# Second layer's attention: all of the first head's weights formed beside the projection, in the room of its raw weights; cached keys loaded a block ahead

## The chip, the cores and the metric

The kernel runs on one core of one Trainium2 chip, in one launch. The metric is the device time in microseconds (us); smaller is better. Before the change the median of three runs is 2865.79 us (2862.54 to 2874.33).

The core's engines are TensorE (PE, matmuls and transposes), VectorE (DVE), ScalarE (ACT) and GpSimd (POOL). SP issues nearly all DMAs here, one after the other. Each engine's instructions run in the order in which the program lists them for that engine, each with the semaphores that it waits for; what stands behind a waiting instruction on its engine waits with it.

## The reference

One step of a streaming encoder for two groups of requests that share weights: a new stream of 16 learned rows and 1024 frames (the prompt), and 32 further frames of a running stream (the sample) with 1024 rows of cache. Two layers, each with a mixer and an MLP of 4096, width 1024, all in float32. The second layer's mixer is forgetting attention with 16 heads of 64:

```python
q, k, v, fl = split_cols(h @ w_in, C_SIZES)          # 1024, 1024, 1024, 16 columns
q = rmsnorm(q.reshape(B_, L, H_C, HEAD_DIM), qn)     # per head
k = rmsnorm(k.reshape(B_, L, H_C, HEAD_DIM), kn)
logf = jax.nn.log_sigmoid((fl + b_f).astype(jnp.float32))
...
s = einsum('bqhd,bkhd->bhqk', q, k) * SCALE + c[q] - c[k]   # c: running sum of logf
p = softmax(where(kpos <= qpos, s, NEG))
o = einsum('bhqk,bkhd->bqhd', p, v)
```

The sample's rows do the same against the 1024 cached keys and values and their own 32. Each output of the projection (new keys, new values, logf) is also an output of the kernel.

## The kernel before, in words

**Precision.** A float32 operand is split into a high part, which TensorE takes at its fast float32 rate, and the rest. `hi_lo` (L62 to L68) does it: a cast on ACT (L64), a subtraction on DVE (L66) or POOL (L68). `mm3` (L71 to L77) then makes a product from three matmuls (high by high, high by low, low by high).

**The end of the first layer.** The MLP of layer 0 ends at about 1324 us in the trace. The norm ahead of the second mixer is computed for four quarters of the 1056 rows; the first three are done inside the MLP, the last stands behind it in the program: squares on ACT (L134), their sums on DVE and POOL (L136, L139), a matmul with the mean (L145), ACT and DVE for the reciprocal root (L148 to L152), the scaling of eight blocks on DVE (L217), and the splitting of each block into high and low (L64, L66, L68), the low part on DVE and POOL by turns. Its scratch tiles live in a pool that is closed directly after (`nms.close()`). Then the pool `fh0` opens, which holds what belongs to head 0 of the attention.

**The projection** (`project_c`, with `project`, L230 to L269): seven groups of columns, one after the other; for each, four loads of raw weights (two blocks of 128 input rows each, L240), their split into `pj_wh` and `pj_wl`, and then nine tiles of rows, each 8 x 3 matmuls into one bank of PSUM. That makes 63 steps. What a step leaves is normed, transposed (L1177) and written to DRAM (`zq`, `zk`, `zv`). The raw weights have a tile of their own, `pj_raw`, three buffers.

**Work beside the projection.** A table gives what is emitted behind which step: behind step 45 the loads of head 0's queries, keys and values (`head_load`, L1418), and behind 56, 58, 60 and 62 its first four blocks of scores with their softmax (`head_scores` L1438, `softmax` L1270). A block of scores is a high matmul (L1452), a low one (L1453) and a mask (L1456), in pieces of a bank's 512 columns or in a wider tile `fx_s`; block number j has 16 + 128 (j + 1) columns. The softmax takes the maximum on DVE (L1275), the exponential on ACT (L1279), and normalises on POOL (L1283). The weights stay in `fx_p0` (four short blocks) and `fx_p1` (six buffers, long blocks).

**The attention** (`fox`, L1487 on): the order on PE is written out by hand. A unit is a head and half of its queries; a step transposes one block of weights (`head_weights`, L1470) and multiplies the values (`head_values`, L1480, L1481); a table sets at which step of head h the scores of head h + 1 are formed, and for head 0 the last four scores are formed beside its first four steps. The sample's attention (`fox_sample`) goes between: per group of four heads, two blocks of 512 cached keys (`fk_c`, loaded at L1318, transposed at L1322), scores (L1334, L1335), cached values. The other engines' order, and SP's order of DMA issues, is set by a scheduler that simulates a timeline.

Of the kernel before, what the change touches and what calls it, by code (L numbers as in the profile page):

```python
# [8 lines left out]
F32 = mybir.dt.float32  # L9
# [9 lines left out]
P = 128  # L19
# [32 lines left out]
class Core:  # L52
# [177 lines left out]
    def project(self, w, cols, sb, hT, lag, part, width=512, bufs=(3, 5)):  # L230
# [3 lines left out]
        for n, (a, b, post, bank) in enumerate(cols):  # L234
            ws = []
            for k in range(0, KB, 2):
                raw = sb.tile([P, 2, width], F32, name="pj_raw", bufs=bufs[0])
# [921 lines left out]
    def project_c(self, hT, beside):  # L1159
        tc, nc, i, o = self.tc, self.nc, self.i, self.o  # L1160
        with tc.tile_pool(name="pc", bufs=2, reuse_waits="tile") as sb, tc.tile_pool(name="pcp", bufs=4, space=PSUM, reuse_waits="tile") as ps:
# [33 lines left out]
            def post_v(h0, nh, gates):  # L1195
                def post(t, r0, m, pp):
# [6 lines left out]
                    if gates:  # L1203
# [30 lines left out]
                                 lambda: sb.tile([P, 512], F32, name="hn_sq"), bufs=(3, 4))  # L1234
            for n, _ in enumerate(steps):
# [3 lines left out]
                if n in beside:  # L1239
                    beside[n]()  # L1240


    def forget_sums(self, sb):
# [9 lines left out]
        for dst, parts in ((self.cp, prompt), (self.cs, sample)):  # L1253
# [9 lines left out]
            for a in range(0, n, n // 2):  # L1263
                hl = [sb.tile([16, 528], F32R, name=f"fs_{x}")[:, :n // 2] for x in "hl"]
                self.hi_lo(d[:, a:a + n // 2], *hl)
                for x in range(2):
                    nc.sync.dma_start(dst[x, :, a:a + n // 2], hl[x].bitcast(F32))


    def softmax(self, sb, pieces, p, n):  # L1270
        nc = self.nc
        nm = sb.tile([P, 2], F32, name="sm_nm", bufs=4)
        den = sb.tile([P, 2], F32, name="sm_den", bufs=4)
        for j, (s, a, b) in enumerate(pieces):
            nc.vector.tensor_reduce(nm[:, j:j + 1], s, axis=AX.X, op=ALU.max, negate=True)  # L1275
        if len(pieces) == 2:
            nc.vector.tensor_tensor(nm[:, 0:1], nm[:, 0:1], nm[:, 1:2], op=ALU.min)
        for j, (s, a, b) in enumerate(pieces):
            nc.scalar.activation(p[:, a:b], s, AF.Exp, bias=nm[:, 0:1], accum_out=den[:, j:j + 1])  # L1279
        if len(pieces) == 2:  # L1280
            nc.vector.tensor_tensor(den[:, 0:1], den[:, 0:1], den[:, 1:2], op=ALU.add)
# [5 lines left out]
    def fox_sample(self, sb, work, ms):  # L1287
# [15 lines left out]

        def keys(g, a, p):
            def go():
# [132 lines left out]
    def head_scores(self, qi, d, sb, ps=None):  # L1438
# [19 lines left out]
        p = sb.tile([P, 1040], F32, name="fx_p1", bufs=6) if qi > 3 else self.fh0.tile([P, 528], F32, name="fx_p0", bufs=4)  # L1458
# [25 lines left out]
    def fox(self, d0, p0, ms, norm):  # L1484
        tc, nc, i = self.tc, self.nc, self.i
        w = i["w_out_c"][0]
        with ExitStack() as st:  # L1487
# [3 lines left out]
            with tc.tile_pool(name="fh", bufs=2, reuse_waits="tile") as sb, tc.manual_schedule(engines={mybir.EngineType.PE}):  # L1491
# [16 lines left out]
                d, pr = {0: d0}, {(0, 0): p0}  # L1508
# [49 lines left out]
                for u, (h, quad) in enumerate(units):  # L1558
                    for t in range(4 * quad + 5):
                        step = 5 * quad + t  # L1560
                        if h == 14 and step == 0:
                            for n, names in enumerate((("fk_c", "fk_h", "fk_l"), ("fx_s", "fx_cs", "fv_c"))):
                                raw, wh, wo = (ssb.tile([P, 2, 512], F32R if x else F32, name=y, bufs=1) for x, y in enumerate(names))
# [3 lines left out]
                        if h == 0 and step < 4:  # L1567
                            scores(0, 4 + step)
# [39 lines left out]
def body(tc, i, o):  # L1608
    C = Core(tc, i, o)
    nc = tc.nc  # L1610
    with ExitStack() as st:
# [109 lines left out]
        with tc.tile_pool(name="fh0", bufs=1, reuse_waits="tile") as fh0:  # L1721
            C.fh0 = fh0
# [103 lines left out]
```

## Time and profile before

| what | before |
|---|---|
| median of three runs | 2865.79 us (2862.54 to 2874.33) |
| profiled execution, its own time | 2855.66 us |
| its span | 2853.9 us |
| PE busy | 2631.2 us, 92% |
| DVE / ACT / POOL busy | 1888.3 / 1264.4 / 560.7 us |
| mean granted clock of PE | 0.963 |
| DMA | 393.77 MB, 138 GB/s on average |
| matmuls of the third projection | 1326.71 to 1643.04 us |

All rows of the trace are from the one profiled execution, in microseconds from its start. The span is the time from its first to its last instruction; 1.8 us of its time lie around that. "Busy" is the sum of the durations of an engine's instructions; "granted clock" is the share of TensorE's full clock that it got in that stretch (1.00 is all of it). In a row of instructions the bracket tells how long the engine was idle before it, and which instruction ended that.

### The profile page before, as it was taken

The page shows a single profiled execution, that of the slowest core. Times are in us where ns is not written, and L with a number is a line of the kernel's source. Part 1 is how long each engine was busy: PE and PEld are TensorE (multiplying, and loading weights), DVE is VectorE, ACT ScalarE, POOL GpSimd, SP SyncE. Part 2 cuts the span into 40 slices and gives each one's busy share as a digit, 9 for nine tenths or more (in the row PEclk, how much of TensorE's full clock was granted, in tenths as well). Part 3 has the DMA queues.
Part 4 walks back from the last instruction along what each step waited for, and adds up shares of the span by engine and source line. Part 5 has one row for each costly group of instructions (what it writes and reads, how often), then busy time and mean ns, then how long its engine had stood idle before and what let it go on. Part 6 is the DMA issues. An engine that isn't in the chain of part 4 may idle for free.

```text
span 2853.9 us, 49119 instructions
## 1 busy us (share of the span) xinstructions
PE 2631.2 (92%) x18391; PEld 2440.6 (86%) x18391; DVE 1888.3 (66%) x3856; ACT 1264.4 (44%) x2820; POOL 560.7 (20%) x611
## 2 busy tenths in 40 slices
PE   5899988879999899999999978999978999899998
PEld 5788966769999799999789856778768999899998
DVE  5934376687676677578643556778888666677553
ACT  4435454243333345445333346666653333335342
POOL 3423354200000010003110244555520000010000
PEclk9999988899999899999999979999988999999999
DMA  5343241143445577544465374344332444486643
GB/s 192 100 134 104 72 140 45 30 120 101 151 129 164 202 231 218 168 134 121 123 193 168 115 176 127 89 101 102 77 91 79 144 147 144 164 274 205 200 138 105
DMA packets 371286, 393.77 MB, mean 138 GB/s; under 512 B 41503, under 2 KB 300280, under 8 KB 369000
## 3 DMA queue, kind: packets, MB, share of 16 engines
q1 hardware_dynamic: 368552, 383.62, 45.6%
q0 software_dynamic: 2496, 7.01, 0.7%
q8 instruction: 145, 2.38, 0.4%
q14 instruction: 93, 0.76, 0.1%
HBM read 263.94 MB, written 125.48 MB: 136 GB/s over the span
## 4 chain that ended last, share of the span: by engine, by line
PE 63%; issue 16%; DVE 9%; DMA 3%; ACT 2%; SPq 1%; POOL 1%; DVEq 0%; ACTq 0%; POOLq 0%
PE bank L75 11%; PE bank L76 11%; PE bank L77 11%; PE mu_y L77 5%; PE mu_y L76 5%; PE mu_y L75 5%; PE bank L1470 2%; PE bank L1480 1%; PE bank L1481 1%; PE fx_s L1452 1%; PE fx_s L1453 1%; DMA md_raw<-in_w_down 1%; PE bank L257 1%; DVE gl_Q L600 1%; PE b L701 1%
## 5 line engine op out<-in xcount | busy, mean ns | idle before, releaser
L75 PE MATMUL bank<-pj_wh,h 128*128 128x384 f32 (+3 forms) x832 | 298.0, 360 | 9.4 <-ACT pj_wh L64 7.0
L77 PE MATMUL bank<-pj_wh,h 128*128 128x384 f32 (+3 forms) x832 | 295.9, 357 | 6.0 <-DVE h L66 4.8
L76 PE MATMUL bank<-pj_wl,h 128*128 128x384 f32 (+3 forms) x832 | 297.3, 358 | 3.5 <-DVE pj_wl L66 3.5
L75 PE MATMUL mu_y<-md_u,md_w 128*128 128x268 f32 (+1 forms) x896 | 259.4, 289 | 26.9 <-ACT md_u L64 26.9
L76 PE MATMUL mu_y<-md_u,md_w 128*128 128x268 f32 (+1 forms) x896 | 257.8, 288 | 2.4 <-DVE md_u L66 2.4
L77 PE MATMUL mu_y<-md_u,md_w 128*128 128x268 f32 (+1 forms) x896 | 257.3, 287 | 0.0
L75 PE MATMUL bank<-md_u,md_w 128*128 128x268 f32 (+1 forms) x896 | 257.1, 287 | 0.0
L77 PE MATMUL bank<-md_u,md_w 128*128 128x268 f32 (+1 forms) x896 | 255.2, 285 | 0.0
L76 PE MATMUL bank<-md_u,md_w 128*128 128x268 f32 (+1 forms) x896 | 254.9, 285 | 0.0
L64 ACT CAST md_u<-md_ur 128x536 fp32r<-128x536 f32 (+1 forms) x224 | 141.1, 635 | 210.7 <-PE mu_y L77 110.7
L66 DVE TENSOR_TENSOR md_u<-md_ur,md_u 128x536 fp32r<-128x536 f32 (+1 forms) x224 | 157.9, 710 | 114.2 <-ACT md_u L64 113.8
L76 PE MATMUL mu_y<-ho_T,mu_w 128*128 128x268 f32 (+1 forms) x768 | 219.8, 286 | 0.2 <-DVE ho_T L66 0.2
L77 PE MATMUL mu_y<-ho_T,mu_w 128*128 128x268 f32 (+1 forms) x768 | 219.9, 286 | 0.0
L75 PE MATMUL mu_y<-ho_T,mu_w 128*128 128x268 f32 (+1 forms) x768 | 219.2, 285 | 0.0
L75 PEld LDWEIGHTS mu_y<-md_u,md_w 128*128 128x128 f32 x896 | 171.1, 191 | 27.4 <-ACT md_u L64 27.3
L66 DVE TENSOR_TENSOR mu_w<-mu_raw,mu_w 128x512 fp32r<-128x512 f32 x160 | 110.0, 688 | 117.0 <-ACT mu_w L64 117.0
L1283 POOL TENSOR_TENSOR fx_p<-fx_p,sm_den 128x144 f32<-128x144 f32 (+7 forms) x128 | 150.6, 1177 | 181.8 <-DVE sm_den L1282 164.7
L64 ACT CAST mu_w<-mu_raw 128x512 fp32r<-128x512 f32 x160 | 99.2, 622 | 188.6 <-PE bank L77 124.6
L75 PEld LDWEIGHTS bank<-pj_wh,h 128*128 128x128 f32 x832 | 158.8, 191 | 22.3 <-ACT pj_wh L64 7.5
L76 PEld LDWEIGHTS mu_y<-md_u,md_w 128*128 128x128 f32 x896 | 170.9, 191 | 3.5 <-DVE md_u L66 3.4
L77 PEld LDWEIGHTS bank<-pj_wh,h 128*128 128x128 f32 x832 | 158.6, 191 | 17.5 <-DVE h L66 5.1
L76 PEld LDWEIGHTS bank<-pj_wl,h 128*128 128x128 f32 x832 | 159.0, 191 | 16.3 <-DVE pj_wl L66 5.2
(538 smaller groups left out, 8096.2 us busy)
## 6 DMA issues: line engine op xcount, KB each, us to landing
md_raw<-in_w_down SPq DMA_DIRECT2D x160, 256.0 KB
mu_raw<-in_w_up SPq DMA_DIRECT2D x64, 512.0 KB
ud<-xT SPq DMA_DIRECT2D x16, 1876.0 KB
md_ur<-ud SPq DMA_DIRECT2D x112, 268.0 KB
ud<-xT SPq DMA_DIRECT2D x16, 1848.0 KB
md_ur<-ud SPq DMA_DIRECT2D x112, 264.0 KB
md_k<-in_w_down SPq DMA_DIRECT2D x16, 1024.0 KB
fh_ka<-zk SPq DMA_DIRECT2D x32, 260.0 KB
```

What stands on the lines that cost most here:

```text
L64: nc.scalar.copy(hi, src)
L66: nc.vector.tensor_tensor(lo, src, hi.bitcast(F32), op=ALU.subtract)
L75: mm(out, ah, bh, start=start, stop=False)
L76: mm(out, ah, bl, start=False, stop=False)
L77: mm(out, al, bh, start=False, stop=stop)
L257: nc.tensor.matmul(*args, start=k == x == 0, stop=k == KB - 1 and x == 1)
L600: eng.tensor_tensor(ov, xv[r, :, :, 1], qv[r, :, :, 1], op=ALU.mult)
L701: nc.tensor.matmul(po[:m, h % 2, h // 2], att[:, h, :m], v[:, P * h:P * h + P], start=True, stop=False)
L1283: nc.gpsimd.tensor_tensor(p[:, :n], p[:, :n], den[:, 0:1].to_broadcast([P, n]), op=ALU.mult)
L1452: nc.tensor.matmul(s[:, a:b], qa[:, qc], ka[:, t0 + a:t0 + b], start=True, stop=False)
L1453: nc.tensor.matmul(s[:, a:b], qb[:, qc], kb[:, t0 + a:t0 + b], start=False, stop=ma >= mb)
L1470: nc.tensor.transpose(pt[:m, P * j:P * j + P], pr[j][:, k0:k0 + m], self.ident)
```

## The change

- `project` may take its raw weights' buffers from outside. The third projection now uses four buffers of head 0's pool (`fx_p10` to `fx_p13`, 1040 columns wide, 1024 used), taken by turns, in place of its own three. The same four buffers then hold head 0's long blocks of weights.
- All eight of head 0's blocks of scores are formed beside the projection, behind steps 50, 52, 54, 55, 57, 59, 61 and 62. The softmax takes up to three pieces for that, since the longest block needs three banks. `fox` no longer forms any of head 0's scores.
- The running sums of the forget gate are split and written in quarters (264 columns) instead of halves, with a smaller tile.
- The block of cached keys is loaded one block ahead, into two buffers; the first load is issued when `fox_sample` begins.

```diff
@@ project
-                raw = sb.tile([P, 2, width], F32, name="pj_raw", bufs=bufs[0])
+                raw = raws() if raws else sb.tile([P, 2, width], F32, name="pj_raw", bufs=bufs[0])
@@ project_c
-                                 lambda: sb.tile([P, 512], F32, name="hn_sq"), bufs=(3, 4))
+                                 lambda: sb.tile([P, 512], F32, name="hn_sq"), bufs=(3, 4),
+                                 raws=lambda: self.weights_tile(self.fh0)[:, 0:1024].rearrange("p (k n) -> p k n", k=2))
+    def weights_tile(self, sb):
+        j = self.turn % (4 if sb is self.fh0 else 6)
+        self.turn += 1
+        return (self.fh0 if j < 4 else sb).tile([P, 1040], F32, name=f"fx_p1{j}", bufs=1)
@@ forget_sums
-            for a in range(0, n, n // 2):
-                hl = [sb.tile([16, 528], F32R, name=f"fs_{x}")[:, :n // 2] for x in "hl"]
-                self.hi_lo(d[:, a:a + n // 2], *hl)
+            for a in range(0, n, n // 4):
+                hl = [sb.tile([16, 264], F32R, name=f"fs_{x}")[:, :n // 4] for x in "hl"]
+                self.hi_lo(d[:, a:a + n // 4], *hl)
                 for x in range(2):
-                    nc.sync.dma_start(dst[x, :, a:a + n // 2], hl[x].bitcast(F32))
+                    nc.sync.dma_start(dst[x, :, a:a + n // 4], hl[x].bitcast(F32))
@@ softmax
-        nm = sb.tile([P, 2], F32, name="sm_nm", bufs=4)
-        den = sb.tile([P, 2], F32, name="sm_den", bufs=4)
+        nm = sb.tile([P, 3], F32, name="sm_nm", bufs=4)
+        den = sb.tile([P, 3], F32, name="sm_den", bufs=4)
...
-        if len(pieces) == 2:
-            nc.vector.tensor_tensor(nm[:, 0:1], nm[:, 0:1], nm[:, 1:2], op=ALU.min)
+        for j in range(1, len(pieces)):
+            nc.vector.tensor_tensor(nm[:, 0:1], nm[:, 0:1], nm[:, j:j + 1], op=ALU.min)
...
@@ fox_sample
+        def cached(g, a):
+            kc = sb.tile([P, 4, 256], F32, name="fk_c", bufs=2)
+            nc.sync.dma_start(kc, i["cache_c_k"][0, 0, 512 * a:512 * a + 512, 4 * g:4 * g + 4].rearrange("(n p) h d -> p n (h d)", p=P))
+            return kc
+
+        ahead = [cached(0, 0)]
...
                 if p == 0:
-                    kc = st["kc"] = sb.tile([P, 4, 256], F32, name="fk_c", bufs=1)
-                    nc.sync.dma_start(kc, i["cache_c_k"][0, 0, 512 * a:512 * a + 512, h0:h0 + 4].rearrange("(n p) h d -> p n (h d)", p=P))
+                    st["kc"] = ahead.pop()
+                    if g + a < 4:
+                        ahead.append(cached(g + a, 1 - a))
@@ head_scores
-        p = sb.tile([P, 1040], F32, name="fx_p1", bufs=6) if qi > 3 else self.fh0.tile([P, 528], F32, name="fx_p0", bufs=4)
+        p = self.weights_tile(sb) if qi > 3 else self.fh0.tile([P, 528], F32, name="fx_p0", bufs=4)
@@ fox
-                d, pr = {0: d0}, {(0, 0): p0}
+                d, pr = {0: d0}, {(0, 0): p0[:4], (0, 1): p0[4:]}
+                self.turn = 4
...
-                        if h == 0 and step < 4:
-                            scores(0, 4 + step)
@@ body
-            C.fh0 = fh0
+            C.fh0, C.turn = fh0, 0
...
-                                  **{56 + 2 * q: lambda q=q: p0.append(C.head_scores(q, d0, fh0)) for q in range(4)}})
+                                  **{n: lambda q=q: p0.append(C.head_scores(q, d0, fh0)) for q, n in enumerate((50, 52, 54, 55, 57, 59, 61, 62))}})
```

How the instructions moved is seen at three places. The rows give the line, the operation, what is written and read, the size of what is written and, in brackets, the semaphores that the instruction waits for: `PE`, `DVE`, `Pool` and `Activation` are raised by those engines, `DMAHW` and `DMASW` by earlier DMAs.

The first is SP at the start of the projection. `md_ur` is the last load of the MLP, `fs_cache` the cached forget gates. Before:

```order
L1058 DMA md_ur<-ud_6543 128x2x268 [waits DMAHW3_49,DVE_49]
L240 DMA pj_raw<-in_w_in_c 128x2x272 [waits PE_49] x2
L240 DMA pj_raw<-in_w_in_c 128x2x272
L1248 DMA fs_cache<-in_cache_c_logf 128x8x16 [waits DVE_49,PE_49]
L240 DMA pj_raw<-in_w_in_c 128x2x272 [waits DMAHW7_49,DVE_49]
```

and of the change:

```order
L1058 DMA md_ur<-ud_6543 128x2x268 [waits DMAHW3_49,DVE_49]
L1255 DMA fs_cache<-in_cache_c_logf 128x8x16 [waits DVE_49,PE_49]
L240 DMA fx_p_14497<-in_w_in_c 128x2x272 [waits DVE_49,PE_49,Pool_49]
L240 DMA fx_p_14503<-in_w_in_c 128x2x272 [waits DVE_49,Pool_49]
L240 DMA fx_p_14509<-in_w_in_c 128x2x272
L240 DMA fx_p_14515<-in_w_in_c 128x2x272
```

The four loads of the first column group now stand behind `fs_cache`, go to the `fx_p` buffers, and the first two wait for DVE and POOL. In the built program the values waited for are those of the last norm's writes of `h`: for the first load DVE's low part of the fifth block and POOL's of the sixth, for the second load DVE's of the seventh and POOL's of the eighth. The buffers lie where the norm's scratch pool was.

The second is PE behind the projection's last matmuls. `L1177` is the transpose of a projected tile, `fh_ka`/`fh_kb` and `fh_qa` are head 0's keys and queries, `fx_p` its weights. Before:

```order
L1177 MATMUL bank<-ident,pc_z 128x128 x4
L1452 MATMUL fx_s<-fh_ka,fh_qa 128x512
L1453 MATMUL fx_s<-fh_kb,fh_qb 128x512
L1452 MATMUL fx_s<-fh_ka,fh_qa 128x144
L1453 MATMUL fx_s<-fh_kb,fh_qb 128x144
L1456 LDWEIGHTS identb
L1456 MATMUL fx_s<-causal,identb 128x128
L1177 MATMUL bank<-ident,pc_z 128x128 x4
L1452 MATMUL bank<-fh_ka,fh_qa 128x512
```

and of the change:

```order
L1177 MATMUL bank<-ident,pc_z 128x128 x4
L1467 MATMUL bank<-fh_ka,fh_qa 128x512
L1468 MATMUL bank<-fh_kb,fh_qb 128x512
L1467 MATMUL bank<-fh_ka,fh_qa 128x400
L1468 MATMUL bank<-fh_kb,fh_qb 128x400
L1471 LDWEIGHTS identb
L1471 MATMUL bank<-causal,identb 128x128
L1177 MATMUL bank<-ident,pc_z 128x128 x4
L1467 MATMUL bank<-fh_ka,fh_qa 128x512
L1468 MATMUL bank<-fh_kb,fh_qb 128x512
L1467 MATMUL bank<-fh_ka,fh_qa 128x512
```

Between the last two tiles' transposes stood score block 4 (656 columns), behind them block 3 and then 5, 6 and 7 among the first weights' transposes; now it is block 6 (912 columns) and then block 7 (1040), and blocks 3, 4 and 5 are ahead of the last projection matmul.

The third is SP ahead of the first block of cached keys. Before (of the eight `fq_s` loads one is shown; head 2's loads stood four rows behind the `fk_c`):

```order
L1294 DMA fx_oc<-in_c_sel 8x128 [waits DMAHW0_49]
L1298 DMA fx_mh<-zk_77 128x8x32 [waits DMAHW1_49,DMASW4_49,DMASW3_49]
L1298 DMA fx_ml<-zk_77 128x8x32 [waits DMAHW2_49]
L1309 DMA fx_cs<-cs 4x1056 [waits DMAHW3_49]
L1314 DMA fq_s<-zq_76 64x32 [waits DMAHW4_49,Pool_49]
...
L1318 DMA fk_c<-in_cache_c_k 128x4x256 [waits DMAHW5_49,PE_49]
```

and of the change:

```order
L1447 DMA fh_qa<-zq_76 64x1024 [waits DMAHW0_49,PE_49]
L1447 DMA fh_qa<-zq_76 64x1024 [waits DMAHW1_49]
L1447 DMA fh_ka<-zk_77 64x1040 [waits DMAHW2_49]
L1447 DMA fh_ka<-zk_77 64x1040 [waits DMAHW3_49]
L1447 DMA fh_qb<-zq_76 64x1024 [waits DMAHW4_49,PE_49]
L1301 DMA fx_oc<-in_c_sel 8x128 [waits DMAHW7_49,DMAHW6_49,DMAHW5_49]
L1305 DMA fx_mh<-zk_77 128x8x32 [waits DMASW4_49,DMASW3_49]
L1305 DMA fx_ml<-zk_77 128x8x32
L1313 DMA fk_c<-in_cache_c_k 128x4x256 [waits DMAHW0_49]
L1323 DMA fx_cs<-cs 4x1056 [waits DMAHW1_49]
```

Five of the loads of head 2 (into head 0's buffers, so behind head 0's last scores on PE) now stand ahead of the first cached block; the samples' queries (`fq_s`) stand behind it, and the second cached block directly behind those.

More of the change, by code (lines that the diff above doesn't have):

```diff
@@ L226, in scaled, with project @@
         return to
-    def project(self, w, cols, sb, hT, lag, part, width=512, bufs=(3, 5)):
+    def project(self, w, cols, sb, hT, lag, part, width=512, bufs=(3, 5), raws=None):
         nc = self.nc
@@ L1562, in fox @@
                             for n, names in enumerate((("fk_c", "fk_h", "fk_l"), ("fx_s", "fx_cs", "fv_c"))):
-                                raw, wh, wo = (ssb.tile([P, 2, 512], F32R if x else F32, name=y, bufs=1) for x, y in enumerate(names))
+                                raw, wh, wo = (ssb.tile([P, 2, 512], F32R if x else F32, name=y, bufs=1 + (y == "fk_c")) for x, y in enumerate(names))
                                 nc.sync.dma_start(raw, w.rearrange("(k p) n -> p k n", p=P)[:, 6:8, 512 * n:512 * n + 512])
```

4 lines of the change are left out of this document (2 added, 2 removed).

## The prediction

> **What bounds the kernel now.** I read the page first (TensorE, PE below, is busy 92% of the span), then the stretches around the third projection, PE's waits there, its rows in order of time, and the chain of waits. First the stretches; the columns are the stretch and its length, then busy time with the instruction count of PE, weight loads, DVE, ACT and POOL, then granted clock, DMA share and GB/s.
>
> ```profile
> 1320.00:1340.00 20.00, 18.09 (x141) 17.57 (x141) 14.76 (x37) 11.23 (x31) 6.80 (x10) 1.00 0.49 140
> 1400.00:1420.00 20.00, 20.00 (x93) 16.41 (x92) 15.02 (x30) 8.79 (x15) 5.34 (x5) 0.96 0.72 201
> 1600.00:1640.00 40.00, 40.00 (x191) 31.90 (x190) 22.35 (x60) 12.74 (x35) 10.10 (x9) 1.00 0.45 137
> 1640.00:1700.00 60.00, 42.27 (x200) 31.44 (x199) 29.51 (x64) 27.11 (x64) 21.96 (x21) 0.74 0.63 159
> 1671.00:1674.00 3.00, 3.00 (x16) 2.77 (x15) 0.90 (x2) 1.86 (x4) 2.11 (x3) 0.50 1.08 281
> 1682.00:1688.00 6.00, 5.67 (x21) 4.19 (x22) 1.47 (x3) 1.36 (x3) 0.00 (x0) 0.50 0.18 58
> ```
>
> Inside the projection PE has no free time (40.00 of 40), so nothing that only makes room there shortens it. The two edges are different: at 1320 PE is nearly full although a norm is still being computed, and after 1640 it is busy for 42.27 of 60 us at a mean clock of 0.74. What it waits for there, in total, times and longest:
>
> ```profile
> PE bank L1322 <- DMA fk_c<-in_cache_c_k: 7.5, 2, 4.1
> PE bank L1177 <- POOL pc_z L1189: 4.2, 1, 4.2
> PE bank L1470 <- POOL fx_p L1283: 4.2, 1, 4.2
> PE fx_s L1452 <- ACT fx_p L1279: 1.7, 2, 1.4
> ```
>
> Four causes, 17.6 us. In PE's own rows (start, duration, what; the bracket is the idle time before it):
>
> ```profile
> 1326.71 0.52 PE L75 MATMUL bank<-pj_wh,h 128*128 128x272 f32 x2 [1.91 <-ACT pj_wh L64]
> ...
> 1643.04 0.60 PE L1177 MATMUL bank<-ident,pc_z 128*128 128x128 f32 x4
> 1643.39 0.48 PE L1452 MATMUL fx_s<-fh_ka,fh_qa 128*128 128x512 f32 x1
> ...
> 1644.12 0.23 PE L1456 MATMUL fx_s<-causal,identb 128*128 128x128 bf16 x1
> 1648.54 1.12 PE L1177 MATMUL bank<-ident,pc_z 128*128 128x128 f32 x4 [4.19 <-POOL pc_z L1189]
> ...
> 1670.66 1.09 PE L1322 MATMUL bank<-ident,fk_c 128*128 128x128 f32 x4 [4.12 <-DMA fk_c<-in_cache_c_k]
> ...
> 1682.33 1.08 PE L1322 MATMUL bank<-ident,fk_c 128*128 128x128 f32 x4 [3.40 <-DMA fk_c<-in_cache_c_k]
> ```
>
> The projection's matmuls run from 1326.71 to 1643.04 (called E below); E to the second block of cached keys is 39.3 us. The change acts on both ends of this.
>
> **The start of the projection: a new wait.** Before, the raw weights have their own three buffers, and three loads leave SP long before they are needed; the fourth is the one that shows what a late load costs:
>
> ```profile
> 1311.49 3.85 SPq L240 DMA_DIRECT2D pj_raw<-in_w_in_c  x3
> 1327.44 0.37 SPq L240 DMA_DIRECT2D pj_raw<-in_w_in_c  x1
> 1330.23 0.65 ACT L64 CAST pj_wh<-pj_raw 128x544 fp32r<-128x544 f32 x1 [2.48 <-DMA pj_raw<-in_w_in_c]
> ```
>
> Issue to cast 2.79 us, cast 0.65. In the changed program the four raw buffers are those of head 0's weights, in the pool that opens where the last norm's pool has just closed. The instruction order shows the consequence: the first of these loads waits for DVE, PE and POOL, and the instructions it waits for are the norm's own writes of h (the low part of the sixth of eight blocks on POOL, of the fifth on DVE) and its mean matmul; the second load waits for the last blocks. So the weights, which need nothing from the norm, are loaded after it. PE has nothing else queued: behind the norm's mean matmul come only projection matmuls. How long the norm takes:
>
> ```profile
> 1310.93 0.48 ACT L148 ACTIVATE nm_a<-mu_y,eps 128x268 f32<-128x268 f32 x1
> 1313.48 1.72 DVE L217 SCALAR_TENSOR_TENSOR nm_t<-xT,gain,nm_y 128x268 f32<-128x268 f32 x4
> 1319.11 1.84 POOL L68 TENSOR_TENSOR h<-nm_t,h 128x268 fp32r<-128x268 f32 x2 [1.23 <-ACT h L64]
> ...
> 1327.43 0.72 DVE L66 TENSOR_TENSOR pj_wl<-pj_raw,pj_wh 128x544 fp32r<-128x544 f32 x1
> 1328.07 0.44 DVE L139 TENSOR_TENSOR nm_acc<-nm_acc,nm_acc 128x268 f32<-128x268 f32 x1
> 1331.22 0.49 ACT L148 ACTIVATE nm_a<-bank,eps 128x268 f32<-128x268 f32 x1 [0.35 <-PE bank L145]
> ```
>
> The first three are the quarter before, undisturbed: 2.55 us from L148 to the first scaling (L217), 7.47 from there to the last low part on POOL (1320.95). The sum L139 stands behind two casts of weights on DVE (0.72 each); without them it comes at about 1326.9, and the mean matmul, which no longer queues behind projection matmuls, at about 1327.4. L148 follows at 1327.9, scaling at 1330.5, the sixth block at 1337.0 (6.5 us on, a little ahead of the last), then load and cast (2.79 + 0.65): first projection matmul at about 1340.5 instead of 1326.71, **13.8 us later**. Bounds: 11.5, if the norm, alone on its engines, runs 2 us faster than its rows; 16, if L139 keeps its time and the loads wait for the last block.
>
> PE is then idle for some 12 us. Its clock after the shorter idle times here was 0.50 for 3.7 us (1670.66 to 1674.4) and for six; half of that is lost, 1.9 to 3.0; I take 2. The Trainium skill ("TensorE: Matmul & The Clock Gate", section "What's actually happening") has half clock after one idle window of about 3.4 us and full clock after as long of sustained work, which gives an estimate of 1.7. The rows bear out the half clock and show a return that takes up to twice as long. The later start takes the projection's own short waits into its slack:
>
> ```profile
> PE bank L75 <- DVE pc_z L278: 2.3, 1, 2.3
> PE bank L1259 <- ACT fs_d L1260: 0.4, 1, 0.4
> ```
>
> These are not late weights, so I credit 1 us of the 2.7 at most. Start: 13.8 + 2 − 1 = **+15** (10.5 to 17.5).
>
> **Inside the projection: nothing.** Four raw buffers instead of three cannot help where PE is full, and the cast pairs keep their four buffers. Sums of the forget gate in quarters: eight more small DMAs of about 0.3 us on SP and four more pairs of casts, under the full PE of 1400:1420. Eight scores' softmax instead of four beside the last columns: 1600:1640 has DVE busy 22.35, ACT 12.74, POOL 10.10 of 40, room for the 10 or so that each gains. If that cover were gone, a projected tile's bank would come late; one such wait is the 4.19 above, and I hold one against the upper end.
>
> **After the projection: less idle.** Scores 3, 4 and 5 move ahead of the last projection matmul, where PE is full and clocked at 1.00. Score 4 above runs 1643.39 to 1644.35; the 784-wide shape at full clock is
>
> ```profile
> 1694.48 0.39 PE L1452 MATMUL fx_s<-fh_ka,fh_qa 128*128 128x512 f32 x1
> ...
> 1695.21 0.23 PE L1456 MATMUL fx_s<-causal,identb 128*128 128x128 bf16 x1
> ```
>
> so 0.8 to 1.0 each: the new end E′ is **2.5 us** later for that reason. After E′ come the last two tiles' transposes, scores 6 and 7, the weights' transposes, and the cached keys. The wait for POOL's pc_z stays. How early can the first cached block come? Before, SP issues it behind everything else of this stage; the chain has
>
> ```profile
> 1648.45 6.18 DMA fh_qb<-zq
> ...
> 1666.83 3.70 DMA fk_c<-in_cache_c_k
> ...
> 1674.59 7.60 DMA fk_c<-in_cache_c_k
> ```
>
> It lands at 1670.6, E + 27.6. After the change it stands ahead of the nine small loads of the samples' queries, but behind five loads of head 2, which wait for score 7 to have read head 0's queries, and it waits itself for the first of these five to land. Score 7 ends at about E′ + 9.8 (4.19 of wait, and transposes and scores at the low clock that follows it, as in the row at 1648.54). A load of head rows took 6.18; that puts the issue at E′ + 16, and 3.70 (alone) to 7.60 (in a full queue) put the landing at E′ + 20 to E′ + 24. Five loads are in flight, so I take 7.60: E′ + 24. From the first to the last instruction before the second block were 8.3 us,
>
> ```profile
> 1678.32 0.61 PE L1470 MATMUL bank<-ident,fx_p 128*128 128x128 f32 x4
> ```
>
> (1670.66 to 1678.93), and the second block, issued right behind the queries, has those 8.3 us for its 7.60, so its 3.40 of idle goes. The second block's transposes come at E′ + 32.3 instead of E + 39.3: 7.0 gained, 2.5 given for the scores. With no idle ahead of the second block the six microseconds at 0.50 from 1682 go too, about 3. Net **−7.5**. Bounds: −12 if the first block lands at E′ + 20; 0 if head 2's loads hold it to E′ + 31 (below). What is late next is ACT: the exponentials of score 7 stand behind a cast of an output weight that comes by DMA:
>
> ```profile
> 1658.48 0.40 ACT L64 CAST oc_h<-oc__19595 128x256 fp32r<-128x256 f32 x1 [4.31 <-DMA oc__19595<-in_w_out_c]
> ```
>
> Its 4.31 us now hold the banks that score 7 filled, and so the transposes behind it; that ends before the cached block lands, and is inside the 24. The heads after these keep their order on PE, and the later blocks' loads showed no idle of PE before.
>
> **Sum.** +15 − 7.5 = **+7.5**. The profiled execution took 2855.66 us, so 2863.2 for such an execution; it lies 10.1 under the median of the three runs (2865.79), so by the median 2873.3.
>
> **Rivals.** Bound of a difference that can be told from none: 0.5%, 14.3 us.
> (a) *Slower: the first cached block stays late.* On SP it stands behind head 2's loads. For it: stretch 1671:1674, in which the same loads run, has the DMA engines full (share 1.08), and fk_c beside them took 7.60 where it took 3.70 alone. Against: the first block is issued some microseconds sooner than before. From a landing at E′ + 31 on, the transition gives nothing and the sum is +15; at E′ + 36 it loses 5, and the sum is +20. That gives 2881 to 2886. Chance 0.21.
> (b) *The new wait costs little, the transition is as worked out.* The raw loads would have to leave SP by about 1329, with the norm's first blocks. Against: the load waits for the sixth block, and L148 alone was at 1331.22. Then −7.5 plus at most 4: 2858 to 2862. Chance 0.12.
> (c) *Faster: all the idle goes.* The 17.6 us of waits and two cold stretches (5 us) vanish and the start costs the low bound: −22.6 + 2.5 + 5 to 10 gives −10 to −15, about 2852. It needs both, and pc_z's wait has no reason to go. Chance 0.04.
> (d) *The change does not do what it says:* the two waits for fk_c only change their names (a bank not freed by score 7's exponentials, or ACT's cast). The transition then gives −1 to −3 and the sum is +12 to +14: 2878 to 2880, still inside the bound. Chance 0.13.
>
> **Numbers.** My forecast, 2873 with its own range 2864 to 2878, has 0.50. Same within 0.5%: 0.50 + 0.12 + 0.13 = 0.75; slower 0.21; faster 0.04. The range 2860 to 2885 takes in (b), (d) and nearly all of (a).
>
> **What would show it.** In the profile after: the first pj_wh matmul at about 1340 with an idle time of some 12 us before it, put down to ACT's cast; four raw loads issued at 1337 to 1339, none before the norm's low parts; a granted clock near 0.5 in the 4 us behind. Projection from first matmul to E′ 318 to 320 us. One wait for fk_c of a few microseconds, none at the second block, and E′ to the second block about 32. I am wrong if raw loads are issued near 1312 or 1327 (then (b)), or if the first fk_c lands beyond E′ + 31 (then (a)), or if PE idles inside the projection for banks.

## The result, and the profile after

| | before | change |
|---|---|---|
| median (5 runs each) | 2864.68 us (2862.54 to 2874.33) | 2877.97 us (2872.53 to 2882.06) |
| ratio to before | | 1.0054 (95%: 1.0034 to 1.0074) |
| profiled execution | 2855.66 us | 2882.06 us |
| its mean granted clock | 0.963 | 0.954 |
| PE busy | 2631.2 us | 2640.6 us |

The change costs 13.3 us by the medians, on the edge of the 0.5% that can be told from nothing; forecast was 7.5 more, with 2873 in a range of 2860 to 2885. A second measurement of the same kernel (first experiment) has 1.0038 (1.0026 to 1.0050). The two profiled executions differ by 26 us, twice as much: that of before lies below all five of its timed runs, that of the change is the slowest of its five. Part of that lies where the programs are the same: the MLP's last matmul starts 8.97 us later, so all times of the change's trace are to be read with that offset.

Before, that matmul is

```profile
1324.52 0.28 PE L77 MATMUL bank<-md_u,md_w 128*128 128x268 f32 x1
```

and PE's rows of the change are

```profile
1333.49 0.28 PE L77 MATMUL bank<-md_u,md_w 128*128 128x268 f32 x1
...
1336.35 0.72 PE L145 MATMUL bank<-nm_acc,mean 128*128 128x268 f32 x2 [2.58 <-DVE nm_acc L139]
1349.02 0.82 PE L75 MATMUL bank<-pj_wh,h 128*128 128x272 f32 x2 [11.95 <-ACT pj_wh L64]
...
1676.78 1.12 PE L1177 MATMUL bank<-ident,pc_z 128*128 128x128 f32 x4 [4.07 <-POOL pc_z L1189]
...
1686.87 1.75 PE L1485 MATMUL bank<-ident,fx_p 128*128 128x128 f32 x7 [5.88 <-ACT fx_p L1286]
...
1696.87 1.09 PE L1337 MATMUL bank<-ident,fk_c 128*128 128x128 f32 x4 [5.41 <-DMA fk_c<-in_cache_c_k]
...
1705.54 0.60 PE L1337 MATMUL bank<-ident,fk_c 128*128 128x128 f32 x4
```

(Lines 1337 and 1485 are 1322 and 1470 of the kernel before.) The projection starts 15.5 us behind the MLP where it was 2.2; the second cached block, last row, has no idle time ahead of it. In the stretches of the change one sees the price in busy time and clock:

```profile
1337.00:1354.00 17.00, 5.05 (x23) 4.92 (x23) 10.60 (x18) 7.20 (x15) 5.25 (x5) 0.50 0.36 106
1600.00:1640.00 40.00, 40.00 (x193) 31.97 (x192) 25.58 (x57) 16.92 (x37) 10.74 (x10) 1.00 0.31 95
1667.00:1727.00 60.00, 42.78 (x223) 32.30 (x222) 31.80 (x73) 29.20 (x70) 23.07 (x21) 0.77 0.79 194
```

The first row is the new hole, 17 us at half clock; the second shows PE still full beside eight scores' softmax (DVE, ACT and POOL are busy 3.2, 4.2 and 0.6 us more than before in that stretch, not the 10 or so of the prediction); the third is the transition, counted from 3 us ahead of the projection's end as 1640 to 1700 was before. It lies 27 us later, 9 of them the offset, and is hardly fuller (42.78 of 60 against 42.27).

For the experiments I use one measure throughout: the start of the weight loads that belong to four matmuls (the MLP's last, the projection's first and last, the first of each cached block). All in us, from each kernel's trace, one execution each:

| kernel | MLP's last to projection's first | projection | its last to first cached block | to second block | ratio to before (95%) |
|---|---|---|---|---|---|
| before | 2.3 | 315.9 | 28.1 | 39.7 | 1 |
| change | 15.6 | 320.6 | 27.2 | 35.8 | 1.0054 (1.0034 to 1.0074) |
| change, again | 16.3 | 320.9 | 26.2 | 34.3 | 1.0038 (1.0026 to 1.0050) |
| raws_only | 15.7 | 318.7 | 29.9 | 41.8 | 1.0048 (1.0035 to 1.0061) |
| start_free | 12.3 | 320.6 | 26.0 | 33.7 | 1.0026 (1.0014 to 1.0038) |
| start_pool | 2.3 | 322.1 | 26.7 | 34.6 | 0.9977 (0.9966 to 0.9988) |
| prefetch_only | 2.3 | 315.7 | 25.2 | 35.6 | 0.9980 (0.9971 to 0.9989) |
| scores_only | 2.3 | 321.8 | 32.2 | 40.6 | 1.0008 (0.9997 to 1.0020) |
| quarters | 2.3 | 318.9 | 28.1 | 39.2 | 1.0002 (0.9990 to 1.0015) |
| pool_keys | 2.3 | 321.7 | 26.5 | 34.4 | 0.9976 (0.9965 to 0.9987) |
| oc_pool | 2.3 | 320.2 | 26.8 | 34.5 | 0.9986 (0.9973 to 0.9998) |
| seven | 2.3 | 320.5 | 24.4 | 33.3 | 0.9982 (0.9970 to 0.9993) |
| seven_fh | 2.3 | 320.3 | 18.9 | 31.8 | 0.9967 (0.9953 to 0.9980) |
| start_pool_fh | 2.3 | 320.1 | 20.0 | 37.5 | 1.0010 (0.9999 to 1.0020) |

One per cent is 28.6 us; an interval of 0.0012 to either side is 3.5 us. The columns show where time goes, and only the ratio says how much: by its columns start_pool reaches the second cached block 1.1 us later than the kernel before, and by its runs it is 6.6 us faster; its profiled execution took 2860.18 us, 5.4 over its median. One stretch of 3.4 us at half clock is worth 1.7 us, and start_pool's trace has one behind the projection's start, at 1328.8, that the trace of seven, with the same start, has not.

### The profile page after: what moved, and what is told of

Its sections match the earlier page's. It is cut to its first block, busy times and chain, and to the rows that moved or that the text cites. A ratio compares the mean times of both kernels' runs of the same rounds, so it can differ in the third digit from the quotient of the medians.

```text
span 2880.3 us, 49154 instructions
## 1 busy us (share of the span) xinstructions
PE 2640.6 (92%) x18377; PEld 2452.9 (85%) x18391; DVE 1891.8 (66%) x3872; ACT 1267.1 (44%) x2832; POOL 567.9 (20%) x611
## 4 chain that ended last, share of the span: by engine, by line
PE 56%; issue 16%; DVE 7%; DMA 3%; ACT 2%; POOL 1%; SPq 0%; DVEq 0%; ACTq 0%; POOLq 0%
PE bank L75 9%; PE bank L77 9%; PE bank L76 9%; PE mu_y L77 5%; PE mu_y L75 5%; PE mu_y L76 5%; PE bank L1485 2%; PE bank L1495 1%; PE bank L1496 1%; PE fx_s L1467 1%; PE fx_s L1468 1%; DMA md_raw<-in_w_down 1%; PE bank L257 1%; DVE xT L873 1%; PE bank L1177 1%
## 5 line engine op out<-in xcount | busy, mean ns | idle before, releaser
L75 PE MATMUL bank<-pj_wh,h 128*128 128x384 f32 (+3 forms) x832 | 300.4, 363 | 19.1 <-ACT pj_wh L64 17.3
L75 PEld LDWEIGHTS bank<-pj_wh,h 128*128 128x128 f32 x832 | 160.2, 193 | 32.2 <-ACT pj_wh L64 18.0
L75 PEld LDWEIGHTS bank<-md_u,md_w 128*128 128x128 f32 x896 | 169.8, 189 | 4.5 <-ACT md_u L64 4.4
```

Source lines behind the costliest of these rows:

```text
L75: mm(out, ah, bh, start=start, stop=False)
```

## The experiments

### The same kernel again, and each half of the change alone

**after_again** is the changed kernel, unaltered.

> The changed kernel once more, unaltered, for a second profile and more times. Theory A (the time is lost at the start of the projection, where raw weights wait for the norm, and partly won back behind it): 2872 to 2882 us; first projection matmul 15 to 16 us after the last matmul of the MLP (2.2 before the change), first cached block some 27 us after the projection's last matmul, second block without idle. Theory B (the loss sits in the attention's clock, which stood at half for 20 us between 1760 and 1850 in the profile of the change, 7 us before it): the half-clock stretches there come again, with about 6 us of loss between the second and the last block of cached keys. By A they do not.

2870.66 us, where before, measured beside it, had 2860.77. The hole at the start and the place of the cached blocks came again. The late loss of theory B did not: from the second cached block's first transposes to the last block's there were 96.3 us in the first trace of the change, 93.6 in this one, and 96.1 before the change. What the first trace lost between 1760 and 1850 belonged to that execution.

**raws_only**: the kernel before with the raw weights in head 0's buffers, and the sums in quarters to make the room.

```diff
-                                 lambda: sb.tile([P, 512], F32, name="hn_sq"), bufs=(3, 4))
+                                 lambda: sb.tile([P, 512], F32, name="hn_sq"), bufs=(3, 4),
+                                 raws=lambda: self.weights_tile(self.fh0)[:, 0:1024].rearrange("p (k n) -> p k n", k=2))
```

> The kernel before with only the raw weights in head 0's four buffers (and the forget gate's sums in quarters, which makes the room); scores and cached keys as before. Theory A: the whole cost of the start and none of the gain: 12 to 17 us slower, 2877 to 2882 us, the first projection matmul 15 to 16 us after the MLP's last. Theory B: 2863 to 2870 us.

2873.51 us, 1.0048: some 14 us slower (10 to 17.5). The move of the raw weights, with the quarters that make the room, costs as much as the whole change, within the error (10.9 us, 7.4 to 14.3, measured beside it). Theory B is out.

**prefetch_only**: the kernel before with cached keys a block ahead, into two buffers.

> The kernel before with only the cached keys a block ahead (two buffers); raw weights and head 0's scores as before. Theory A: the two waits for the cached block (7.5 us) and the slow clock behind the second shrink; on SP the first block now stands ahead of the nine small loads of queries, the second ahead of head 2's loads: 4 to 9 us faster, 2856 to 2861 us. Rival C (the transition is set by the exponentials and the banks, not by this load): PE waits there for something else, 2863 to 2867 us.

2854.78 us, 0.9980: some 6 us faster (3.1 to 8.3). PE's waits between 1640 and 1690, in total, times and longest:

```profile
PE bank L1478 <- POOL fx_p L1283: 5.5, 2, 4.1
PE bank L1177 <- POOL pc_z L1189: 4.2, 1, 4.2
PE fx_s L1460 <- ACT fx_p L1279: 1.7, 2, 1.4
PE bank L1342 <- DMA fh_qa<-zq: 1.3, 1, 1.3
```

No wait for a cached block is left; 7.5 us went, and about 1.3 came back at each of two other places.

### Is the start's cost the wait for the norm?

**start_free** gives head 0's key, query and value tiles the first room of the pool, so that the raw weights lie behind them and no longer where the norm's scratch was.

```diff
             C.fh0, C.turn = fh0, 0
+            C.first = C.head_tiles(fh0)
```

> The change, but head 0's key, query and value tiles take the first room of the pool, so that the raw weights' buffers no longer lie where the norm's scratch was; nothing else is altered. Theory A: first projection matmul again 2 to 3 us after the MLP's last, no cold clock behind it; 15 us come off, so 2858 to 2864 us, at or a little under the kernel before. Theory B: the start costs next to nothing in the end, because later waits take it up, and the time stays at 2872 to 2880 us.

2868.84 us, 1.0026: only a few us of the expected 15 came off, and theory A seemed to fall. The trace of this kernel shows why it need not. Its SP rows have the first loads at

```profile
1327.47 21.05 SPq L240 DMA_DIRECT2D fx_p<-in_w_in_c  x8
```

its ACT rows the norm's last casts and the weights' first,

```profile
1342.99 1.23 ACT L64 CAST h<-nm_t 128x268 fp32r<-128x268 f32 x3 [0.49 <-DVE nm_t L217]
1344.12 2.28 ACT L64 CAST pj_wh<-fx_p 128x544 fp32r<-128x544 f32 x4
```

and its PE rows the projection's first matmul:

```profile
1344.82 0.82 PE L75 MATMUL bank<-pj_wh,h 128*128 128x272 f32 x2 [8.50 <-ACT pj_wh L64]
```

The loads leave 5 us ahead of the MLP's last matmul (1332.67 here) and wait for nothing of the norm, but ACT casts the weights only behind the last blocks of h, because ACT's order has them there; PE's order has the norm's mean matmul ahead of the projection's first, too. So the wait is one cause, and the order that the scheduler made of the buffers' place is another, of about 10 us, which stays when the wait is gone.

**start_pool** takes the four buffers from a pool of their own, opened behind head 0's pool; nothing else of the change is altered.

```diff
-        with tc.tile_pool(name="fh0", bufs=1, reuse_waits="tile") as fh0:
-            C.fh0, C.turn = fh0, 0
+        with tc.tile_pool(name="fh0", bufs=1, reuse_waits="tile") as fh0, tc.tile_pool(name="fhr", bufs=1, reuse_waits="tile") as fhr:
+            C.fh0, C.fhr, C.turn = fh0, fhr, 0
...
-        return (self.fh0 if j < 4 else sb).tile([P, 1040], F32, name=f"fx_p1{j}", bufs=1)
+        return (self.fhr if j < 4 else sb).tile([P, 1040], F32, name=f"fx_p1{j}", bufs=1)
```

> The change with the four raw-weight buffers in a pool of their own, opened behind head 0's pool, so that they lie over early parts of the MLP's weights instead of the norm's scratch; the instruction order has the four loads ahead of the cached forget gates again and the projection's first matmuls ahead of the norm's mean matmul, as before the change. Theory A (the raw weights' late casts are the whole loss; moving only the buffers was not enough because ACT's order still had the casts behind the norm): first projection matmul 2 to 3 us after the MLP's last, no half clock there, and the difference between the change (+10.9 us) and the raw weights alone (+13.7) is left, with the cold clock gone: 3 to 6 us under the kernel before, 2855 to 2858 us. Theory B (the slower start is only the first place of a loss that comes anyway): 2866 us or more.

2854.83 us, 0.9977: 6.6 us faster than before (3.4 to 9.7), and by the ratios some 17 us faster than the change (1.0038 in the second measurement). SP's rows of it at the start,

```profile
1312.40 4.82 SPq L240 DMA_DIRECT2D fx_p<-in_w_in_c  x4
1319.80 0.37 SPq L1255 DMA_DIRECT2D fs_cache<-in_cache_c_logf  x1
```

and PE's rows at the projection's first matmul and behind its last:

```profile
1327.61 0.52 PE L75 MATMUL bank<-pj_wh,h 128*128 128x272 f32 x2 [1.90 <-ACT pj_wh L64]
...
1667.17 1.76 PE L1485 MATMUL bank<-ident,fx_p 128*128 128x128 f32 x7 [6.14 <-ACT fx_p L1286]
1676.47 1.09 PE L1337 MATMUL bank<-ident,fk_c 128*128 128x128 f32 x4 [4.71 <-DMA fk_c<-in_cache_c_k]
```

All four loads leave ahead of the forget gates' cache, and the projection starts at once. Theory A holds in its wider form: the whole loss sits in the place of the raw weights. Why the scheduler orders the two differently was not found: in start_free, too, the loads waited for nothing of the norm, but there they stood behind the forget gates' cache and left at 1327.47. start_pool changes the pool and, with it, the place of the buffers, and which of the two decides is not shown.

### Which part gains, and what sets the transition

**scores_only** is start_pool without the prefetch.

> As the kernel with the buffers in their own pool, but each block of cached keys loaded when it is needed, into one buffer, as before the change: what is left is all of head 0's scores beside the projection. Theory A: the cached block is then on SP behind head 2's loads and all the small loads, so its wait grows and eats what the scores gave: between 2 us faster and 5 us slower than before, 2859 to 2866 us. Theory D (the scores are what gains, the prefetch adds nothing to it): as fast as with the prefetch, 2855 to 2858 us.

2865.40 us, 1.0008: nothing gained by the scores that the timing can tell. PE's waits between 1640 and 1690:

```profile
PE bank L1334 <- DMA fk_c<-in_cache_c_k: 10.4, 1, 10.4
PE bank L1482 <- ACT fx_p L1286: 6.0, 1, 6.0
PE bank L1177 <- POOL pc_z L1189: 4.9, 2, 4.1
```

With the scores ahead, PE reaches the first cached block sooner, the block itself comes 4 us later (32.2 against 28.1), and PE waits for it longer. Against start_pool the prefetch is worth 0.3%, about 9 us; against the kernel before it was worth 6. The scores, with the prefetch, add nothing that can be told: 0.9977 against 0.9980. Both kernels with the scores also have the sums in quarters; a gain by the scores as large as the quarters' cost, next, is not excluded.

**quarters** is the kernel before with only the forget gate's sums in quarters.

> The kernel before with only the forget gate's sums in quarters instead of halves. The prediction had this at nothing. The profiles of all kernels that have it show PE waiting 1.6 us for fs_d where the kernel before waits 0.4, and two half-clock windows (6.8 us) around 1400 where it had one (3.4), together some 3 us: 2 to 4 us slower if that is its cost, no difference if the prediction was right and the windows come from the later start.

2861.10 us, 1.0002: nothing in the measured time. Its one profile has the projection 3.0 us longer, with this wait in it:

```profile
PE bank L1259 <- ACT fs_d L1260: 3.1, 1, 3.1
```

The interval (0.9990 to 1.0015) leaves room for that, so its cost is between nothing and 4 us. In the traces of the other kernels with quarters this wait is 1.6 us, in that of before 0.4.

**pool_keys**: start_pool, with the first cached block issued by GpSimd.

```diff
-            nc.sync.dma_start(kc, i["cache_c_k"]...)
+            (nc.sync if g + a else nc.gpsimd).dma_start(kc, i["cache_c_k"]...)
```

> As the kernel with the buffers in their own pool, but the first block of cached keys is issued by GpSimd, so that it neither stands behind head 2's five loads on SP nor waits for the load eight back there. Theory A (the first cached block's landing sets the end of the transition): it lands 3 to 6 us earlier, PE's wait of 5.4 us for it shrinks to 0 to 2, and the time falls by 2 to 5 us against that kernel: 2851 to 2855 us. Theory E (ACT sets it: the exponentials of score 7 behind the cast of the output weight): the wait moves to another name and the time stays within 1.5 us.

2853.75 us, 0.9976: no change. The block was issued only 0.6 us sooner behind the projection's last matmul (19.0 against 19.6); on GpSimd it stood behind an output weight's low part, which waited 4.83 us for ACT's cast, and behind a clearing of fq_s, which waited 1.08 us for a load of head rows:

```profile
1665.45 0.72 POOL L68 TENSOR_TENSOR oc_l<-oc__19642,oc_h 128x256 fp32r<-128x256 f32 x1 [4.83 <-ACT oc_h L64]
1667.26 0.53 POOL L1308 MEMSET fq_s<- 128x512 f32 x1 [1.08 <-DMA fh_qa<-zq]
1668.11 0.81 POOL L1313 DMA_DIRECT2D fk_c<-in_cache_c_k  x1 [0.33 <-issue]
```

So this run tells nothing between A and E; the next does.

**oc_pool**: pool_keys, with the output projection's weights cast by GpSimd instead of ACT.

> As the kernel in which GpSimd issues the first cached block, and the output projection's weights are cast by GpSimd instead of ACT, so that ACT's exponentials of score 7 no longer stand behind a cast that waits for its load. Theory E: the 5.9 us wait of the weights' transposes for these exponentials goes, 3 to 6 us come off against that kernel. Theory A: the cached block still lands when it did, PE waits longer for it, and the time stays within 1.5 us or gets worse by GpSimd's extra casts (32 casts, about 0.7 us each, off PE's path).

2856.38 us, 0.9986. The waits:

```profile
PE bank L1341 <- DMA fk_c<-in_cache_c_k: 9.6, 1, 9.6
PE bank L1181 <- POOL pc_z L1193: 4.9, 2, 4.1
PE bank L1489 <- ACT fx_p L1290: 1.3, 1, 1.3
```

The wait for ACT fell from 6.1 in pool_keys to 1.3, the one for the block rose from 4.5 to 9.6, and the time did not fall: it was idle time inside a wait that ends later. Theory A: the cached block sets this stage.

**seven**: start_pool with score 7 formed in the attention's fourth step, as before the change.

> The buffers in their own pool, cached keys a block ahead, but score 7 of head 0 is formed in the attention's fourth step again, as before the change; scores 0 to 6 stay beside the projection. In the instruction order both cached blocks now stand ahead of head 2's loads on SP, because those wait for score 7. Theory A (head 2's loads ahead of the cached block set the transition's length): the first cached block comes 3 to 6 us earlier behind the projection's last matmul (26.7 us in the kernel with all eight), and the time falls by 3 to 6 us against it: 2849 to 2853 us where the kernel before has 2861 to 2863. Rival F (the gain there is taken back by the exponentials, the projected tile on GpSimd or the clock): within 1.5 us of it.

2855.78 us, 0.9982: as fast as start_pool, not faster. The cached block now stands ahead of head 2's loads, and comes 2.3 us earlier, not 3 to 6:

```profile
1677.05 1.09 PE L1337 MATMUL bank<-ident,fk_c 128*128 128x128 f32 x4 [11.11 <-DMA fk_c<-in_cache_c_k]
```

Now one wait holds nearly all. SP issued the block at 1672.35, behind the loads of the samples' new keys. Its buffer lies over the projection's last tiles, which must be written out first; that this is what kept it back is an assumption here, and the next experiment moves the buffer.

**seven_fh**: seven, with the first of the two cached-key buffers taken from the heads' pool, which lies elsewhere.

```diff
-            kc = sb.tile([P, 4, 256], F32, name="fk_c", bufs=2)
+            kc = (sb if a else first).tile([P, 4, 256], F32, name="fk_c", bufs=1)
...
-                smp = self.fox_sample(ssb, [x.rearrange("p a b -> p (a b)") for x in mixes[1]], ms)
+                smp = self.fox_sample(ssb, [x.rearrange("p a b -> p (a b)") for x in mixes[1]], ms, sb)
```

> As the kernel with scores 0 to 6 beside the projection, but the first of the two cached-key buffers is taken from the heads' pool, which does not lie over the projection's last tiles; in the instruction order the first cached block now leaves SP ahead of head 1's loads. In that kernel all of PE's idle time behind the projection had become one wait of 11.1 us for this block. Theory A: the wait goes, the cached block is there before PE wants it, and PE runs on until the queries' and forget sums' small loads are late: 4 to 8 us off that kernel, 2847 to 2852 us where the kernel before has 2861. Rival G: the queries of the samples, still behind head 1's loads and the samples' new keys, are then waited for as long, and the time stays within 2 us of it, 2854 to 2857.

2852.20 us, where before, measured beside it, had 2861.54: 0.9967 (0.9953 to 0.9980), 9.4 us faster than before. It is the lowest ratio of all, but the intervals of seven and of start_pool overlap with it: against seven it is 4 us, where Rival G allowed 2. The block leaves SP ahead of head 1's loads and is there 18.9 us behind the projection; the waits that are left are others:

```profile
PE bank L1337 <- DVE fh_pl L66: 5.6, 1, 5.6
PE bank L1177 <- POOL pc_z L1189: 4.9, 2, 4.1
PE bank L1485 <- POOL fx_p L1290: 2.8, 1, 2.8
```

**start_pool_fh**: the same buffer, with all eight scores beside the projection.

> The same buffer placement with all eight scores beside the projection. The waits there were 6.1 us for score 7's exponentials (behind an output weight's load on ACT) and 4.7 us for the cached block. Theory A: the second goes, the first stays: 2 to 5 us off the kernel with the buffers in their own pool, 2850 to 2853 us. Rival G: the wait moves to the samples' queries, within 1.5 us of it, about 2854 to 2856.

2865.13 us, 1.0010: 9 us slower than start_pool, which neither theory had. The waits for the block and for ACT's exponentials (6.1 to 1.3) shrank, and this came:

```profile
PE bank L1349 <- DMA fq_s<-zq: 6.7, 1, 6.7
PE bank L1177 <- POOL pc_z L1189: 4.9, 2, 4.1
PE bank L1495 <- ACT fh_ph L64: 2.5, 1, 2.5
```

Rival G's mechanism, the wait that moves to the samples' queries, is there, and it costs more than what it replaces: the second block comes at 37.5 us instead of 34.6. In this kernel SP issues head 2's loads from 1664.50, ahead of all the small ones, and the eight loads of queries only from 1676.30; in seven_fh the queries' loads leave from 1667.48, and most of head 2's behind them.

## Why the prediction was right, and where it was off

**The start, +15, held in every step.** With 8.97 us of offset: the mean matmul was to come at 1336.4 (1327.4 on the clock of before) and came at 1336.35; the first raw load at 1346.0 and came at 1345.52; the first projection matmul at 1349.5 and came at 1349.02. In the change's rows SP issues the loads

```profile
1345.52 4.61 SPq L240 DMA_DIRECT2D fx_p<-in_w_in_c  x5
```

in the midst of the norm's last low parts on POOL,

```profile
1344.23 1.80 POOL L68 TENSOR_TENSOR h<-nm_t,h 128x268 fp32r<-128x268 f32 x2 [0.82 <-ACT h L64]
```

and ACT's cast waits for the first:

```profile
1348.33 0.64 ACT L64 CAST pj_wh<-fx_p 128x544 fp32r<-128x544 f32 x1 [3.35 <-DMA fx_p<-in_w_in_c]
```

Delay 13.3 by the trace, 13.8 predicted; half clock to about 1354, 5 us beyond the first matmul, so 2.5 lost where I took 2. The Trainium skill's 3.4 us of sustained work to full clock ("TensorE: Matmul & The Clock Gate", "What's actually happening") would have given an estimate of 1.7; the row sides with the longer stretches. What was incomplete is the cause. I named the wait; start_free, in which the wait is gone, shows that ACT's and PE's orders hold 10 of the 13.4 us of delay by themselves. The number came out because both end at the norm; that is luck as far as the order goes.

**The credit of 1 us inside the projection did not come, and "nothing" for its other edits was a little low.** The projection grew by 4.8 us. Of that, 2.5 were forecast for the three scores; the clock gave more than the 2 that I took. PE worked some 10 us at half clock in it, 5.2 from 1349.0 to 1354.2 and 5.3 between 1419 and 1426, where it had 3.4 around 1400 before, and half of the difference is 3.5. The norm's mean matmul, 0.6 us, now stands ahead of it. PE's waits there did not shrink (pc_z and fs_d, 2.7 us before and 3.3 now), so the 1 us was not taken into slack. Together these come to 6; where the last microsecond went is not placed. PE full at 1600 to 1640 was right. The quarters cost up to 3 us in a profile and nothing that the timing can tell.

**The transition, −7.5, was right in kind; its size is not settled.** The wait at the second block went, as said. The first block was mis-sized: predicted 24 us behind the projection, measured 26 to 27. The step that failed is "that puts the issue at E′ + 16". The chain of the change has

```profile
1675.48 7.16 DMA fh_kb<-zk
1682.71 0.37 SPq L1182
...
1683.48 5.90 DMA fh_qa<-zq
1689.40 4.09 SPq L1313
```

Ahead of head 2's loads stood the writes of the projection's last tile, and they waited for an earlier load of head 1; so head 2's first load left at E′ + 13.4 (E′ is 1670.1) instead of about E′ + 10. It landed in 5.90 (6.18 predicted), the cached block's issue began at E′ + 19.3, and the block was there 7.5 us later (7.60 predicted). The second block came at 34 to 36 us instead of 32, where 39.7 was; 4 to 5.5 us gained for 7.0 predicted, less the scores' 2.5 and plus what the clock gave. PE's time from E to the second block, before and with the change, shows what the shortening is made of:

```profile
1643.00:1682.30 39.30, 22.00 (x98) 16.22 (x96) 18.19 (x43) 16.62 (x41) 17.82 (x17) 0.69 0.88 218
1670.00:1705.50 35.50, 19.29 (x83) 14.25 (x82) 14.35 (x36) 12.10 (x32) 11.05 (x12) 0.62 0.92 222
```

PE's idle time fell only from 17.3 to 16.2 us; the other 2.7 are scores that were moved, and paid for, ahead of E′. Two measurements give the whole term, and they differ. What start_pool gained over the kernel before, 6.6 us (3.4 to 9.7), is this term with the start taken away, and −7.5 lies within it. What the change gained over raws_only, 2.9 us (2873.51 to 2870.66, with some 5 us of error), is the term with the start in place. Not seen in the sum: as far as the timing can tell, the scores' part of it is nothing and the prefetch's is all.

**ACT's hold was named as next late, and was.** ACT's row in the change:

```profile
1685.26 0.40 ACT L64 CAST oc_h<-oc__19639 128x256 fp32r<-128x256 f32 x1 [6.74 <-DMA oc__19639<-in_w_out_c]
```

It cost PE 5.9 us of idle, and oc_pool, in the kernel with the buffers in their own pool, shows that there it was inside the wait for the cached block, as the prediction had it.

**The sum.** +7.5 predicted, 10 to 13 by the medians of the two measurements, inside the range of the forecast's own case (2864 to 2878), the first of them at its very edge (2877.97). Of the rivals, (a) did not come: the cached block landed short of E′ + 31, though 3 us later than thought; (b) and (c) did not either. Of (d) a part came: one of PE's two long waits before the second block is now for score 7's exponentials behind ACT's cast, as (d) names it, and its +12 to +14 is as near to the two measurements as +7.5 is. So the number does not tell the forecast's own case from (d).

## What to carry to other kernels

A buffer that is taken from a later stage's pool inherits what that pool lies over: look up, in the instruction order, what the first load into it waits for and what it now stands behind, before counting what the buffer saves. Removing the wait was not enough here, since the other engines still stood in the same order; a pool of its own gave the old order back. Look at the order again after such a move. And when work is moved ahead of a wait, ask who ends that wait: eight scores moved forward bought nothing that could be told, without the transfer moved ahead (1.0008) or with it (0.9977 against 0.9980). Where the transfer left earliest, one score left behind was better than none (0.9967 against 1.0010), and there most of the loads that wait for it stood behind the small ones that PE wanted first.

## What was not expected of the hardware

- The granted clock stays at half although PE works for much of the time. A stretch of the change, with PE busy for half of it, all at 0.50:

```profile
1675.00:1702.00 27.00, 13.93 (x54) 10.55 (x55) 9.22 (x23) 7.98 (x23) 8.16 (x8) 0.50 0.92 207
```

  So a wait's price there is not its length alone: the work between two waits of 4 to 6 us also runs at half.
- Issuing one load can itself take long: SP needed 4.09 us for the first cached block's issue in the change (1689.40 above) and 3.51 at the same place in start_pool, where the later blocks' issues in the change took 0.37 to 0.59. The DMA engines were full then (share 1.14 from 1689 to 1694 in the change); whether that is the cause was not tested.
